# Six query column tiles by pairs of seven products, the layer input's pair operands made beside v, attention results in their own SBUF tiles

## The chip, the cores and the metric

The kernel runs on one core of a Trainium2 chip. The metric is the device time of one execution in microseconds (us). The engines are named as in the profile: PE multiplies matrices (PEld is its weight load), DVE and ACT do elementwise work and read PE's results out of PSUM, POOL does small elementwise work and issues some transfers, SP issues most transfers. All five run their own instruction list in order and wait for each other by semaphores.

## The reference

One layer of a decoder on 512 prompt tokens and 8 x 8 sample tokens, so 576 token columns in all. What matters here is the first half of the layer, up to the attention:

```python
h = _rmsnorm(x, norm1_g) * (1.0 + sc1) + sh1
proj = h @ w_in
b_gate, c_gate, xa, q, k, v, ga, gb = jnp.split(proj, cuts, axis=-1)
u = c_gate * xa
uc, new_conv = _causal_conv(u, conv_buf, conv_w)
ya = (b_gate * uc) @ w_conv_out
...
s = jnp.einsum('...qhgd,...khd->...hgqk', q, k).astype(jnp.float32) * (HEAD_DIM ** -0.5)
s = s - _alibi_slopes()[:, :, None, None] * dist[..., None, None, :, :]
s = jnp.where(valid[..., None, None, :, :], s, NEG_INF)
m = jnp.maximum(jnp.max(s, axis=-1, keepdims=True), sink)
p = jnp.exp(s - m)
p = p / (jnp.sum(p, axis=-1, keepdims=True) + jnp.exp(sink - m))
o = jnp.einsum('...hgqk,...khd->...qhgd', p.astype(v.dtype), v)
...
yb = o @ w_attn_out
mixed = jax.nn.sigmoid(ga) * ya + jax.nn.sigmoid(gb) * yb
x = x + g1 * (mixed @ w_mix_out)
```

D_MODEL is 1024. `w_in` is 1024 x 6656: 8 column tiles of 128 each for b_gate, c_gate, xa and q, 2 each for k and v, 8 each for ga and gb. There are 16 query heads of 64 in 4 groups, one group for each of 4 key heads, and the window is 128. The second half of the layer (norm, up-projection, convolution, down-projection, final norm) is not touched.

## The kernel before

**Tiles.** Activations lie with channels on the 128 partitions and the 576 tokens along the free axis: `h` is 8 tiles (k = 0 to 7) of 128 x 576. To keep float32 accuracy each operand is split in a high and a low part (ACT copies the high part, DVE subtracts it), and each product of tiles is three matmuls: high by high, high by low, low by high.

**Two ways to multiply.** `product` (L218) makes one column tile of an output: 8 k-steps x 3 passes x 2 token groups (256 and 320 tokens) = 48 matmuls of 288 columns on average, into one two-bank PSUM buffer of the pool `mm` (2 buffers). `pair_product` (L449) makes two column tiles together by Winograd's form of Strassen's scheme, on a 2 x 2 blocking of the weights (contraction halves by column tiles) and of the activations (contraction halves by token halves of 288): seven block products of 4 k-steps x 3 passes = 84 matmuls of 288 columns, in place of 2 x 48 = 96. Its parts run in this order over three PSUM regions X, Y, Z: `a0.x00` into X, `s1.n1` into Z, `s2.t2` into Y, `a1.x10` into X, `s3.n3` into Y, `s4.x11` into Z, `b1.n4` into Y. Between them ACT writes -X into Y before `s2.t2` may add to it, copies Z to a tile `p5`, and writes -Y into Z. It needs sums and differences of activation halves (`PairOperands`, L243: `sums` is four DVE operations of 128 x 288, `high` is ACT's part, `low` DVE's; the block names `n1`, `t2`, `n4`, `n3` are such sums) and of weight tiles (`pair_weights`, L394: `sums1` and `sums2` are four DVE operations of 128 x 512, then three full splits and a half one).

**Stages around the change.** k and the first query tile are multiplied while the norm is still being made. Then v is multiplied token tile by token tile (L848 to L856, 5 x 24 matmuls of 256 columns, PSUM from the pool `aux`, 4 buffers). Then query tile 1, and then a loop over `PLAIN` (L1431), six rounds called `at` 0 to 5: each multiplies a c_gate tile (`c`) and an xa tile with `product`, and DVE multiplies the two results (`pad`). Rounds 1 to 3 first multiply two query tiles each with `product`, one after the other, and `queries` (L887) takes each out of PSUM: two ACT copies `q`, two DVE operations `low`, and POOL's transfers `q<-low` that bring the other 64 partitions. Rounds 4 and 5 make the pair operands of `h` (`operands`, L1426), and their last block `n3` overwrites the second token half of four tiles of `h`, which can be done only after the last plain product, beside the first pair job (`jobs[0].before`). From then on all column tiles are multiplied by pairs (`jobs`).

**Attention.** It is a generator, `attention` (L1151), whose steps are called from `tick` inside the products at a rate of steps for each k-step (`filler`). One unit is a key head by a block of 128 queries: `prompt_scores` (PE), softmax (DVE for mask, maximum, sums and scaling; ACT for the exponentials), `prompt_turn` two units later (PE transposes, ACT copies `pt`), `prompt_values` for two units together (PE, and ACT copies into `ot`, two large tiles of four k-tiles each). A unit of a head starts only when its queries are made and 8 ticks have passed.

**Order.** PE's instructions keep the program's order from the attention on (`pinned`). DVE, ACT, POOL and SP are ordered when the program is built, by a timeline of that build, except in the stages that pin them; they then run in that order on the chip. Tiles come from a pool of 57 equal slots (`slot`); weights from 4 buffers `raw`, 5 buffers `whi` and 5 `wlo`. A new tile waits until the buffer's last reader is done.

Of the kernel before, what the change touches and what calls it, by code (L numbers as in the profile page):

```python
# [16 lines left out]
P = 128  # L17
# [16 lines left out]
CACHE_AT = 15, 16  # L34
# [38 lines left out]
def step_kernel(ctx: ExitStack, tc: tile.TileContext, ins: dict, outs: list):  # L73
# [222 lines left out]

    class BesideOperands:
# [96 lines left out]
    def pair_weights(ra, rb, moved=""):  # L394
# [22 lines left out]
        def s3_slots():  # L417
            return slot("wh", F32R, [P, 4, P]), slot("wl", F32R, [P, 4, P])
# [30 lines left out]
    def pair_product(w, x, steps, out_a0, out_a1, out_b0, out_b1):  # L449
# [3 lines left out]
        X, Z = (aux()[:, :HT] for _ in range(2))  # L453
        Y = halves(mmps())[1][:, :HT]
# [359 lines left out]
    q0 = kT.pop(0)  # L814

# [71 lines left out]
    def queries(t, ps=None):  # L887

        scale = HD**-0.5 if ps is None else 1.0
# [35 lines left out]
    queries(0, q0)  # L925
    queries(1)
    con = slot("con", shape=[P, 520])
    nc.sync.dma_start(con[:, 0:256], ins["consts"][:, CND : CND + 256])
    nd = con[:, 0:256]
# [39 lines left out]
    ot = [wp.tile([P, 4, NT], F32, tag="oh", name=nm("o"), bufs=2) for _ in range(2)]  # L969
# [86 lines left out]
    def decode_values(q, s, cV):  # L1056
# [12 lines left out]
        c = slice(512 + 32 * q, 512 + 32 * q + 32)  # L1069
        for j in range(2):  # L1070
# [12 lines left out]
            for hf in range(2):  # L1083
                src = O[HALF[hf], :P].rearrange("p (b x g t) -> p x g b t", b=4, x=2, g=2)
                dst = ot[j][:, 2 * hf : 2 * hf + 2, c]
# [45 lines left out]
    def prompt_values(parts):  # L1131
        O = aux()
        for u, (hd, i, pts) in enumerate(parts):
# [11 lines left out]
        for u, (hd, i, pts) in enumerate(parts):  # L1145
            nc.scalar.copy(
                ot[hd // 2][:, 2 * (hd % 2) : 2 * (hd % 2) + 2, i * P : i * P + P],
                O[:, 256 * u : 256 * u + 256].rearrange("p (g c) -> p g c", g=2),
            )
# [137 lines left out]
    ycv, gcv, made, made_g = {}, {}, {}, {}  # L1287
    wco, wao = ins["w_conv_out"][0], ins["w_attn_out"][0]

    class Job:  # L1290
# [9 lines left out]
        def prepare(self, moved="", late=False):  # L1300
            self.w, t = pair_weights(*self.raws, moved=moved)
# [122 lines left out]
    hp = [PairOperands(h, kp, made, xn) for kp in range(4)]  # L1424

    def operands(kp):  # L1426
        hp[kp].sums()
        hp[kp].high()
        hp[kp].low()

    for at, m in enumerate(PLAIN):  # L1431
        if at in (4, 5):
# [58 lines left out]
    def g_list(names):  # L1491
        return [g_at(int(n[0]), n[1:]) for n in names.split()]

    jobs[0].before = {2: [op.n3 for op in hp]}
    jobs[1].before = {3: [lambda: inner[6]()]}
# [10 lines left out]
        },  # L1506
        12: {0: "1third_low 3third 2third_low", 2: "3third_low"},
# [731 lines left out]
```

## Time and profile before

| | |
|---|---|
| time, median of 3 runs | 962.5 us (962.43 to 963.56) |
| profiled execution: its own time | 963.13 us |
| profiled execution: span from first to last instruction | 961.0 us |
| granted TensorE clock | 0.998 |
| v, window 52.70 to 67.30 us | 14.60 us |
| query tile 1 and the six rounds of `PLAIN`, window 67.30 to 228.40 us | 161.10 us |
| all pair jobs and the rest, from 228.40 us | 732.6 us |

The program runs on one core, so there is no second die to compare with. A window row gives, for a stretch of the span, the length, then busy time and instruction count of PE, PEld, DVE, ACT and POOL, the granted clock (1.00 is full speed), and what the transfers did. PE's matmuls overlap in their pipeline: a row that says 300 ns for one matmul is its latency, while a stream of them starts one every 0.13 us. So the length of a stretch divided by the number of its matmuls is the price of one, not the mean in the table of groups.

### The profile page before, as it was taken

What the parts mean: (1) busy time and instruction counts of PE and PEld (TensorE: products, weight loads), DVE (VectorE), ACT (ScalarE), POOL (GpSimd) and SP (SyncE); (2) the same over time, 40 slices, a digit from 0 to 9 for tenths busy, and PEclk for the clock granted to TensorE, in tenths of its full rate; (3) what the DMA queues carried; (4) which work ended last, traced back from release to release, by engine and by line L of the source; (5) the groups of instructions that cost most, each with busy time, mean ns of one, the idle gap of its engine ahead of it and who ended that gap; (6) DMA issues with size and microseconds to landing.
All of it is one profiled execution on the core that took longest, in us unless ns stands there. A gap on an engine that the chain in (4) does not pass through costs nothing.

```text
span 961.0 us, 18726 instructions
## 1 busy us (share of the span) xinstructions
PE 946.4 (98%) x7326; PEld 912.7 (95%) x7326; DVE 711.9 (74%) x1331; ACT 539.1 (56%) x1020; POOL 132.3 (14%) x309
## 2 busy tenths in 40 slices
PE   6999999999999999999999999999999999999997
PEld 5799999998999989999889999999999999999997
DVE  4656787697966767776677688995559998868874
ACT  5454665556665446875335567563226565546664
POOL 2122112201211011210001131100000001101110
PEclk9999999999999999999999999999999999999999
DMA  9985332423655767899885732332323333328542
GB/s 275 330 255 147 90 86 71 131 90 96 155 147 178 244 219 199 219 250 285 283 291 119 174 97 66 89 109 67 107 88 92 89 89 101 92 72 172 138 95 99
DMA packets 182650, 144.08 MB, mean 150 GB/s; under 512 B 7688, under 2 KB 162124, under 8 KB 182274
## 3 DMA queue, kind: packets, MB, share of 16 engines
q1 hardware_dynamic: 172546, 111.72, 38.8%
q0 software_dynamic: 9872, 30.92, 14.0%
q8 instruction: 57, 0.93, 0.4%
q14 instruction: 31, 0.25, 0.1%
q10 hardware_dynamic: 144, 0.26, 0.1%
HBM read 113.89 MB, written 12.07 MB: 131 GB/s over the span
## 4 chain that ended last, share of the span: by engine, by line
PE 95%; DMA 3%; SPq 1%; ACT 0%; DVE 0%; issue 0%; DVEq 0%
PE mm L112 55%; PE aux L112 37%; PE aux L1234 2%; DMA ad<-in_w_ada 1%; PE aux L1137 1%; DMA raw<-in_w_in 1%; SPq L497 1%; DMA q<-low 0%; ACT whi L112 0%; ACT wlo L112 0%; DVE cs L504 0%; ACT hh L112 0%; DVE hl L112 0%; DVE yo L112 0%; ACT acc L112 0%
## 5 line engine op out<-in xcount | busy, mean ns | idle before, releaser
L112 ACT ACTIVATE whi<-raw 128x1024 fp32r<-128x1024 f32 (+3 forms) x183 | 185.6, 1022 | 108.7 <-PE mm L112 51.9
L112 DVE TENSOR_TENSOR wlo<-raw,whi 128x1024 fp32r<-128x1024 f32 (+2 forms) x160 | 188.8, 1186 | 49.0 <-ACT whi L112 48.1
L112 PE MATMUL mm<-hh,whi 128*128 128x256 f32 x336 | 74.3, 302 | 0.5 <-ACT hh L112 0.5
L112 PE MATMUL mm<-hh,wlo 128*128 128x256 f32 x336 | 71.7, 295 | 0.0
L112 PE MATMUL mm<-hl,whi 128*128 128x256 f32 x336 | 70.8, 295 | 0.1
L112 PE MATMUL aux<-2h,whi 128*128 128x288 f32 (+2 forms) x232 | 68.6, 296 | 0.0
L112 PE MATMUL aux<-2l,whi 128*128 128x288 f32 (+2 forms) x232 | 68.5, 295 | 0.0
L112 PE MATMUL aux<-2h,wlo 128*128 128x288 f32 (+2 forms) x232 | 68.3, 294 | 0.0
L112 DVE TENSOR_TENSOR raw<-raw 128x512 f32<-128x512 f32 x82 | 57.5, 701 | 2.6
L112 PEld LDWEIGHTS mm<-hh,whi 128*128 128x128 f32 x336 | 55.1, 189 | 1.8 <-ACT hh L112 1.0
L112 PEld LDWEIGHTS mm<-hl,whi 128*128 128x128 f32 x336 | 55.6, 188 | 0.7 <-DVE hl L112 0.5
L112 PEld LDWEIGHTS mm<-hh,wlo 128*128 128x128 f32 x336 | 56.2, 188 | 0.0
L112 PE MATMUL aux<-hh,whi 128*128 128x288 f32 (+2 forms) x184 | 54.0, 301 | 0.0
L112 PE MATMUL aux<-hl,whi 128*128 128x288 f32 (+2 forms) x184 | 53.0, 295 | 0.0
L112 PE MATMUL aux<-hh,wlo 128*128 128x288 f32 (+2 forms) x184 | 52.9, 295 | 0.0
L112 PE MATMUL mm<-th,whi 128*128 128x288 f32 x164 | 49.2, 300 | 0.0
L112 PE MATMUL mm<-nh,whi 128*128 128x288 f32 x164 | 49.0, 299 | 0.0
L112 PE MATMUL mm<-th,wlo 128*128 128x288 f32 x164 | 48.6, 296 | 0.0
L112 PE MATMUL aux<-th,wlo 128*128 128x288 f32 x164 | 48.5, 296 | 0.0
L112 PE MATMUL aux<-th,whi 128*128 128x288 f32 x164 | 48.5, 296 | 0.0
L112 PE MATMUL mm<-nh,wlo 128*128 128x288 f32 x164 | 48.5, 296 | 0.0
L112 PE MATMUL mm<-nl,whi 128*128 128x288 f32 x164 | 48.4, 295 | 0.0
(374 smaller groups left out, 3012.3 us busy)
## 6 DMA issues: line engine op xcount, KB each, us to landing
raw<-in_w_in SPq DMA_DIRECT2D x52, 512.0 KB, 5.0
raw<-in_w_up SPq DMA_DIRECT2D x44, 512.0 KB, 3.8
ada<-in_w_ada SPq DMA_DIRECT2D x64, 256.0 KB, 5.5
wlo<-raw POOLq DMA_DIRECT2D x17, 512.0 KB, 4.6
ad<-in_w_ada SPq DMA_DIRECT2D x32, 256.0 KB, 6.6
raw<-in_w_down SPq DMA_DIRECT2D x16, 512.0 KB, 4.2
sg_dram<-sg POOLq DMA_DIRECT2D x16, 288.0 KB, 4.9
gt<-sg_dram SPq DMA_DIRECT2D x16, 288.0 KB, 6.0
```

The costliest lines, as they stand in the source:

```text
L112: done = getattr(self.engine, name)(*args, **kwargs)
L497: return tc.keep_in_program_order(nc.sync.dma_start(dst, src))
L1137: done = nc.tensor.matmul(O[HALF[par], c], vt(i - nkt + 1 + kt)[:, hd * 64 : hd * 64 + 64], pts[kt][:, par * 256 : par * 256 + 256], start ...
L1234: done = nc.tensor.matmul(ps[32 * j : 32 * j + 32, :], cT[:, k, :], cols[k][j], start=(k == 1), stop=(k == NK - 2),)
```

## The change

- **Queries by pairs.** In rounds 1 to 3 (`Q_PAIRS`) the two query tiles are made by one `pair_product` of 84 matmuls in place of two `product` calls of 48. Its weights (`q_job`) are loaded and prepared in the round before, inside that round's xa product. It takes X and Y from the pool `mm` (`apart=True`) and Z from `aux`, leaving the attention the other three `aux` buffers. The results go to two SBUF tiles `qt` (ACT copies the first halves, DVE adds `p5` for the second halves), and `queries` reads them there. The attention's rate is 0.2 steps for a tick inside a pair and 0.32 after it, in place of 0.3.
- **Operands of `h` beside v.** `EarlyOperands` makes all of `sums`, `high` and `low`, one of four k-pairs in each of v's token tiles 1 to 4. `n3` has its own tiles now, because the plain products still need `h`. The operations that rounds 4 and 5 and the first pair job had for it are gone.
- **Results in SBUF tiles of their own.** The high and low parts of the operands `n1` and `t2` (`t`) take the two large tiles that the attention's results had. The results `ot` are now eight slots, copied by 128 columns instead of two times 128 at once; the sample tokens' results go to one tile `od` and POOL copies them into `ot` before the output projection.
- **Small things.** ACT loads the exponential's table before v (`act.activation(first, ...)`). The mask constant `nd` lies in the unused half of v's last tile. The sample cache is loaded two units later (`CACHE_AT`). Some operand making of a later stage is moved by one part in `plan`.

```diff
-CACHE_AT = 15, 16
+Q_PAIRS = (1,2,3,)
+OPS_AT = 1, 2, 3, 4
+CACHE_AT = 17,18
...
+    class EarlyOperands(PairOperands):
+        def high(self):
+            made, (h0, l0), (h1, l1) = self.made, *self.x
+            if "t" not in made:
+                made["t"] = [wp.tile([P, 4, NT], F32R, tag="oh", name=nm("t"), bufs=2) for _ in range(2)]
+            self.th, self.tl = (x[:, self.kp, :] for x in made["t"])
+            act.activation(self.th, self.t, AF.Copy)
+            if self.kp % 2 == 0:
+                for n in ("n4", "n3"):
+                    made[n] = slot(n + "h", F32R), slot(n + "l", F32R)
+            a, b = slice(0, HT), slice(HT, NT)
+            at = (a, b)[self.kp % 2]
+            nh, nl = made["n4"]
+            self.nh, self.nl = nh[:, at], nl[:, at]
+            self.n3h, self.n3l = (x[:, at] for x in made["n3"])
+            act.activation(self.nh, self.r[0][:, a], AF.Copy)
+            act.activation(self.n3h, self.r[0][:, b], AF.Copy)
...
+        def all_early(self):
+            self.sums()
+            self.high()
+            self.low()
+
+        def low(self):
+            for lo, src, hi in (
+                (self.tl, self.t, self.th), (self.nl, self.r[0][:, :HT], self.nh),
+                (self.n3l, self.r[0][:, HT:], self.n3h),
+            ):
+                dve.tensor_tensor(out=lo, in0=src, in1=hi.bitcast(F32), op=ALU.subtract)
...
-        X, Z = (aux()[:, :HT] for _ in range(2))
-        Y = halves(mmps())[1][:, :HT]
+        X, Y = (halves(mmps())[1][:, :HT] if apart or n else aux()[:, :HT] for n in range(2))
+        Z = aux()[:, :HT]
...
     q0 = kT.pop(0)
+    act.activation(first, q0[:, 0:1], AF.Exp, scale=0.0)
...
+    made = {}
     for i in range(5):
+        if i in OPS_AT:
+            EarlyOperands(h, OPS_AT.index(i), made, xn).all_early()
         ps = aux()
...
         for u, (hd, i, pts) in enumerate(parts):
-            nc.scalar.copy(
-                ot[hd // 2][:, 2 * (hd % 2) : 2 * (hd % 2) + 2, i * P : i * P + P],
-                O[:, 256 * u : 256 * u + 256].rearrange("p (g c) -> p g c", g=2),
-            )
+            for g in range(2):
+                at = 256 * u + P * g
+                nc.scalar.copy(ot[2 * hd + g][:, i * P : i * P + P], O[:, at : at + P])
...
+        w = weights(kpm(w_in, 1024 + m * P), NK)
         if 1 <= at <= 3:
             key_parts(at)
-            for t in (2 * at, 2 * at + 1):
-                queries(t)
-        w = weights(kpm(w_in, 1024 + m * P), NK)
-        if at in (4, 5):
-            operands(2 * at - 8)
+            if at in Q_PAIRS:
+                qt = [slot("qt") for _ in range(2)]
+                filler[1] = .2
+                pair_product(q_job.w, made["op"], {}, *copy_outs(qt), True)
+                filler[1] = .32
+            for n in range(2):
+                queries(2 * at + n, qt[n] if at in Q_PAIRS else None)
...
         w = weights(kpm(w_in, 2048 + m * P), NK)
-        if at in (4, 5):
-            operands(2 * at - 7)
         steps = {}
+        if at + 1 in Q_PAIRS:
+            q_job = Job(w_in, Q0 + (2 * at + 2) * P, None, None)
+            q_job.load()
+            fs = [f for x in q_job.prepare("").values() for f in x]
+            for k, n in [(0, 2), (1, 1), (2, 1), (3, 1), (4, 2), (5, 1), (6, 1), (7, 1)]:
+                steps[k], fs = fs[:n], fs[n:]
...
-    jobs[0].before = {2: [op.n3 for op in hp]}
-    jobs[1].before = {3: [lambda: inner[6]()]}
+    jobs[1].before = {4: [lambda: inner[6]()]}
...
     def part_o(n):
         for k in range(len(o), n):
-            o.append(split_slot(ot[k // 4][:, k % 4, :], "o"))
+            nc.gpsimd.tensor_copy(out=sv(ot[k]), in_=od[0][:, k, :])
+            o.append(split_slot(ot[k], "o"))
```

In the built order, names carry a number for each buffer. The first place is ACT around the first pair, between the xa product of round 0 (`mm_1006` before, `mm_1062` now) and what follows it. `whi` of round 1's weights, `y` and `kh` are the convolution's first tap and the next key head; the rows `s,den` are the exponentials of one attention unit; `mm_1191` is X, `mm_1192` is Y, `aux_1193` is Z. Before:

```order
L984 ACTIVATE s_1025,den_1045<-s_1025,nmx_1041 128x128 x2
L984 ACTIVATE s_1026,den_1045<-s_1026,nmx_1041 128x128 x2
L990 ACTIVATE es_1046<-es_1046 128x4
L112 ACTIVATE whi_1588<-raw_1586 128x1024
L112 ACTIVATE y_1096<-pad_1089,parT 128x592
L112 ACTIVATE kh_1100<-kT_663 64x512
L112 ACTIVATE whi_1702<-raw_1700 128x1024
L896 ACTIVATE q_1230<-mm_1112 64x512
```

Now:

```order
L114 ACTIVATE whi_1179<-raw_1177 128x1024
L114 ACTIVATE y_1173<-pad_1166,parT 128x592
L114 ACTIVATE kh_1183<-kT_663 64x512
L1028 ACTIVATE s_1091,den_1111<-s_1091,nmx_1107 128x128 x2
L1028 ACTIVATE s_1092,den_1111<-s_1092,nmx_1107 128x128 x2
L114 ACTIVATE mm_1192<-mm_1191 128x288
L1034 ACTIVATE es_1112<-es_1112 128x4
L114 COPY p_1194<-aux_1193 128x288
L114 ACTIVATE aux_1193<-mm_1192 128x288
```

The exponentials of the first attention unit moved behind the weight split, `y` and `kh`, and the pair's -X into Y stands behind all of these.

The second place is DVE while v and then query tile 1 are multiplied. `tw` and the changed `xn` are the operands' sums, `t`, `n4l` and `n3l` their low parts, `wlo_1055` and `wlo_1003` are the same low part of round 0's xa weights. Before:

```order
L112 TENSOR_TENSOR wlo_854<-raw_851,whi_853 128x1024
L112 TENSOR_TENSOR wlo_942<-raw_939,whi_941 128x1024
L112 TENSOR_TENSOR wlo_1003<-raw_1000,whi_1002 128x1024
L112 TENSOR_TENSOR wlo_1109<-raw_1106,whi_1108 128x1024
L112 TENSOR_TENSOR wlo_1243<-raw_1240,whi_1242 128x1024
L112 TENSOR_TENSOR kl_835<-kT_663,kh_834 64x512
```

Now:

```order
L114 TENSOR_TENSOR wlo_994<-raw_991,whi_993 128x1024
L114 TENSOR_TENSOR tw_713<-xn_304 128x288
L114 TENSOR_TENSOR tw_713<-xn_469,tw_713 128x288
L114 TENSOR_TENSOR xn_304<-xn_304,xn_469 128x288
L114 TENSOR_TENSOR xn_304<-xn_469,tw_713 128x288
L114 TENSOR_TENSOR wlo_1055<-raw_1052,whi_1054 128x1024
L114 TENSOR_TENSOR t_719<-tw_713,t_718 128x576
L114 TENSOR_TENSOR n4l_722<-xn_304,n4h_721 128x288
L114 TENSOR_TENSOR n3l_724<-xn_304,n3h_723 128x288
L114 TENSOR_TENSOR tw_756<-xn_306 128x288
```

The sums of the first k-pair come before round 0's xa weights and the rest follows them, ahead of the key's and the queries' low parts (`kl`, `low`).

More of the change, by code (lines that the diff above doesn't have):

```diff
@@ L417, in s3_slots @@
         def s3_slots():
+            if not narrow:
+                return [x[:, 0:4, :] for x in tiles()]
             return slot("wh", F32R, [P, 4, P]), slot("wl", F32R, [P, 4, P])
@@ L885, in key_parts, with queries @@
         KS[hd] = kh, kl
-    def queries(t, ps=None):
-        scale = HD**-0.5 if ps is None else 1.0
+    def queries(t, ps=None, scale=HD**-0.5):
         if ps is None:
@@ L968, in step_kernel @@
     pinned.append(pe)
-    ot = [wp.tile([P, 4, NT], F32, tag="oh", name=nm("o"), bufs=2) for _ in range(2)]
+    ot = []
+    od = []
     def softmax_steps(s, n, sinks, nsinks, w):
@@ L1068, in decode_values @@
         yield False
-        c = slice(512 + 32 * q, 512 + 32 * q + 32)
+        c = slice(32 * q, 32 * q + 32)
+        if not od:
+            od.append(slot("od", shape=[P, NK, 64]))
         for j in range(2):
@@ L1132, in prompt_values @@
         O = aux()
+        while len(ot) < 2 * parts[-1][0] + 2:
+            ot.append(slot("ot"))
         for u, (hd, i, pts) in enumerate(parts):
@@ L1300, in prepare @@
         def prepare(self, moved="", late=False):
-            self.w, t = pair_weights(*self.raws, moved=moved)
+            self.w, t = pair_weights(*self.raws, moved=moved, narrow=self.outs is not None)
             order = {0: "sums1 ah al", 1: "bh bl", 3: "dh dl sums2", 4: "ch", 5: "cl"}
@@ L1422, in step_kernel @@
     jobs += [Job(wco, m * P, made_g, lambda m=m: conv_outs(m)) for m in range(0, NK, 2)]
[L1424 to L1429, printed above, removed]
     for at, m in enumerate(PLAIN):
```

22 lines of the change are left out of this document (13 added, 9 removed), and 2 rows, old and new, of the table plan.

## The prediction

> **What bounds the kernel now.** I read the page's first part and its chain that ended last, then the windows by stage, then the chain in order of time.
>
> ```profile
> span 961.0 us, 18726 instructions
> PE 946.4 (98%) x7326; PEld 912.7 (95%) x7326; DVE 711.9 (74%) x1331; ACT 539.1 (56%) x1020; POOL 132.3 (14%) x309
> PE 95%; DMA 3%; SPq 1%; ACT 0%; DVE 0%; issue 0%; DVEq 0%
> ```
>
> The last chain is 95% PE work. Busy time alone would not prove that, as matmuls overlap, but the chain says that PE seldom waited. The windows show it for the stages that the change touches:
>
> ```profile
> 52.70:67.30 14.60, 14.60 (x125) 14.60 (x124) 4.28 (x4) 7.24 (x16) 0.54 (x1) 1.00 0.93 260
> 67.30:228.40 161.10, 160.78 (x1256) 153.55 (x1254) 121.53 (x327) 93.25 (x248) 28.46 (x62) 1.00 0.36 103
> ```
>
> The first row is v, the second query tile 1 and the six rounds. PE is busy for all but 0.32 us of 175.7 us, at full granted clock (1.00). DVE is busy for 125.8 us (4.28 + 121.53), 72%, ACT for 100.5 us. So here a matmul that is taken away shortens the kernel by its full price, as long as DVE and ACT deliver in time; a faster DVE or ACT brings nothing.
>
> **The price of the matmuls.** The chain in order of time has two plain products without anything between them, and the steady pairs of the up-projection:
>
> ```profile
> 67.35 12.67 PE mm L112 x96
> ...
> 741.71 3.17 PE aux L112 x24
> ...
> 752.84 3.19 PE aux L112 x24
> ...
> 763.98 3.18 PE aux L112 x24
> ```
>
> Two products take 12.67 us for 96 matmuls, 0.132 us each. A piece of 24 `aux` matmuls is the first two parts of a pair, X and Z, so from one such piece to the next is one pair: 11.13 us (752.84 - 741.71) and 11.14. That is 84 matmuls at 0.1325 us, with nothing lost between the parts. One pair for two products saves 12.67 - 11.13 = 1.54 us, three save 4.62 us. The attention's own PE work is the same in both kernels, and in the built order the last prompt values stand just before the first pair job in both, so nothing of it is pushed into a later stage.
>
> **The operands beside v.** Their parts and those of the weights have these rows (groups from 52 to 245 us, the last three from 228 to 450 us; behind the bar busy us, then the mean of one in ns):
>
> ```profile
> L112 DVE TENSOR_TENSOR wlo<-raw,whi 128x1024 fp32r<-128x1024 f32 x25 | 30.5, 1223 | 18.0 <-ACT whi L112 17.8
> L112 ACT ACTIVATE whi<-raw 128x1024 fp32r<-128x1024 f32 x26 | 27.3, 1057 | 40.9 <-PE mm L112 25.9 <-issue 6.2 <-DMA raw<-in_w_in 3.9
> L112 DVE TENSOR_TENSOR tl<-tw,th 128x576 fp32r<-128x576 f32 x4 | 3.0, 751 | 3.5 <-ACT th L112 3.3
> L112 DVE TENSOR_TENSOR raw<-raw 128x512 f32<-128x512 f32 x4 | 2.8, 690 | 0.1
> L112 ACT ACTIVATE th<-tw 128x576 fp32r<-128x576 f32 x4 | 2.7, 683 | 0.9 <-PE aux L112 0.9
> L112 DVE TENSOR_TENSOR tw<-xn,tw 128x288 f32<-128x288 f32 x4 | 1.8, 454 | 0.1
> L112 ACT ACTIVATE nh<-xn 128x288 fp32r<-128x288 f32 x4 | 1.7, 430 | 0.0
> L1146 ACT COPY o<-aux 128x256 f32<-128x256 f32 x16 | 5.2, 375 | 9.5 <-PE aux L1137 9.5
> ...
> L112 ACT ACTIVATE wh<-s 128x512 fp32r<-128x512 f32 x18 | 11.2, 623 | 0.0
> L112 ACT ACTIVATE mm<-aux 128x288 f32<-128x288 f32 x18 | 7.2, 397 | 12.3 <-PE aux L112 12.3
> L112 ACT COPY p<-aux 128x288 f32<-128x288 f32 x18 | 7.0, 390 | 3.0 <-PE aux L112 2.7
> ```
>
> Sums, 16 x 0.454 = 7.3 us, and low parts, 4 x 0.751 + 8 x 0.454 = 6.6 us, make 13.9 us on DVE; high parts, 4 x 0.683 + 8 x 0.430 = 6.2 us on ACT. The cover is v and query tile 1 with the next PE work, until 86 us:
>
> ```profile
> 67.30:86.00 18.70, 18.70 (x145) 18.70 (x144) 10.40 (x25) 9.70 (x21) 8.09 (x16) 1.00 0.71 196
> ```
>
> DVE is idle there for 10.3 us in v and 8.3 us after it, 18.6 us, ACT for 16.4 us. The operands fit, and the first pair needs them at about 87 us. Behind them in DVE's order are the low parts of the key and of two query tiles; until the last of these is done, the xa product cannot have its PSUM buffer.
>
> ```profile
> 61.27 1.23 DVE L112 TENSOR_TENSOR wlo<-raw,whi 128x1024 fp32r<-128x1024 f32 x1 [5.33 <-ACT whi L112]
> ...
> 78.76 0.22 DVE L907 TENSOR_SCALAR qX<-mm 64x64 f32<-64x64 f32 x1
> ...
> 87.42 0.69 DVE L112 TENSOR_TENSOR pad<-mm,c 128x512 f32<-128x512 f32 x1 [0.51 <-PE mm L112]
> 88.03 0.86 DVE L994 TENSOR_SCALAR s<-s,den 128x128 f32<-128x128 f32 x4
> 88.81 0.22 DVE L112 TENSOR_TENSOR pad<-mm,c 128x64 f32<-128x64 f32 x1
> ```
>
> Before, the last of them ended at 78.98 us and the product began at 80.02 (67.35 + 12.67). Now four sums fill DVE's 5.33 us of idle time, and from 61.27 on stand two splits (2.4 us), the rest of the operands (13.9 - 1.8) and five low parts of about 0.69 with some small ones (4.2): 80.0 us by full durations. Successive DVE operations overlap by about 0.08 us (`pad` at 87.42 lasts 0.69, the next starts at 88.03); over some 30 of them that is 2.4 us, so 77.6. Between 0 and 0.1 us for PE; I take 0. ACT's table load goes from the attention to a time when ACT waits for a transfer; PE waits for it in neither place.
>
> **The weights and the results.** Each pair adds on DVE 4 x 0.690 (sums) + 0.690 (half low part; no row of this stage, so the same size) + 1.223 (three low parts for two), 4.7 us, and 2 x 0.454 for the second halves of `qt`. On ACT it adds 1.057 + 0.623, and 5 x 0.39 (-X, -Y, `p5`, two copies), 3.6 us. `n3` comes from the pair job: 4 x 0.45 us on each. The results' copies go from 16 x 0.375 to 32 copies of half the width. Half width is not in this row; between 0.19 (proportional) and 0.375, they add 0 to 6 us on ACT, and I take 3. DVE then has 125.8 + 3 x 5.6 + 1.8 = 144.4 us in 175.7 - 4.6 = 171.1 us, 84%; ACT 100.5 + 10.9 + 1.8 + 3 = 116.2, 68%. Both still fit, but DVE has 27 us of slack in place of 50. Averages do not settle it; the hand-overs do.
>
> **The hand-over inside a pair.** This is the one new place where PE waits for ACT at short notice. Y takes the `mm` buffer in which the xa product has just ended. PE may add `s2.t2` to Y only when DVE has read that product (`pad`), and ACT has written -X there. Until then PE has X, 8 score matmuls and Z. Rows of round 0 on ACT, and eight score matmuls from the chain:
>
> ```profile
> 85.93 0.39 ACT L984 ACTIVATE s<-s,nmx 128x128 f32<-128x128 f32 x1
> ...
> 87.20 1.06 ACT L112 ACTIVATE whi<-raw 128x1024 fp32r<-128x1024 f32 x1 [0.70 <-ACT es L990]
> 89.12 0.79 ACT L112 ACTIVATE y<-pad,parT 128x592 f32<-128x592 f32 x1 [0.86 <-DVE pad L112]
> 89.94 0.63 ACT L112 ACTIVATE kh<-kT 64x512 fp32r<-64x512 f32 x1
> ...
> 88.18 0.94 PE aux L112 x8
> ```
>
> PE's cover is 12 x 0.1325 + 0.94 + 12 x 0.1325 = 4.1 us. ACT's list in that time, by the built order of the first pair: `whi` 1.06 (its buffer is freed by the xa product's end), `y` 0.79, `kh` 0.63, four exponentials of 128 at 0.39, -X 0.40: 4.4 us. `pad` itself, 0.69 + 0.22 with nothing between its two parts now, is done within `whi`. PE waits 0.3 us. The second pair has the same list, the third no exponentials ahead. So 0.6 us in all. The bounds: 0 if the overlap of successive ACT instructions is worth 0.3 us; and up to 1.5 us for each pair if DVE comes to `pad` one low part (1.223 us) later than I think, 4.5 us in all. I take 0.6, near the low end, since DVE's order puts no long operation between the xa product's end and `pad`.
>
> The Trainium skill speaks against this (Perfetto Trace Analysis, Matmuls): independent matmul groups should rotate through different PSUM banks, so that emptying one overlaps the next group. A pair that takes both `mm` buffers gives up that rotation once for each pair. In this trace the steady pairs, which take one of their three regions from there, lose nothing (11.13 us above); what the rule would cost here is in the third rival.
>
> **The queries' transfer.** Before, head 3 was the only PE wait in the six rounds:
>
> ```profile
> PE aux L112 <- DMA q<-low: 0.3, 1, 0.3
> ...
> L896 ACT ACTIVATE q<-mm x14: 572/590/596, 74.4 to 176.3; 64x512 fp32r<-64x512 f32 x14
> L899 DVE SCALAR_TENSOR_TENSOR low<-mm,q x14: 672/688/695, 77.3 to 177.9; 64x512 fp32r<-64x512 f32 x14
> ...
> DMA to landing us min/median/max: 2.2/2.7/6.9
> ...
> 178.24 4.48 DMA q<-low
> ```
>
> From ACT's last copy at 176.3 to the landing at 182.7 are 6.4 us. Now both tiles of a head come at once, 4 x 0.590 on ACT and 4 x 0.688 on DVE in place of half of each, about 2.6 us more: 9.0 us. In the built order PE has between the pair and the head's first scores a c_gate product and 18 to 24 matmuls of the xa product (66 to 72 x 0.132 = 8.7 to 9.5 us), and 16 to 21 of the attention's, at 0.94 / 8 each 1.9 to 2.5 us: 11 us or more. That covers it, and the old wait of 0.3 us goes.
>
> **The sum.** Against the profiled execution's own 963.13 us (span 961.0, 2.1 us around it): -4.62 (matmuls) - 0.3 (old wait) + 0.6 (hand-over) = -4.3, so 958.8. That execution lies 0.6 us above the median of the three runs, 962.5; by the median 958.2. I say 958.5 us.
>
> **The rivals.** The third needs two rows of the softmax:
>
> ```profile
> L984 ACT ACTIVATE s<-s,nmx 128x256 f32<-128x256 f32 x50 | 24.9, 501 | 4.5 <-DVE nmx L978 2.8 <-DVE den L992 1.6
> L975 DVE TENSOR_REDUCE nmx<-s 128x2 f32<-128x512 f32 x26 | 17.0, 678 | 0.0
> ```
>
> 1. *Half of it is given back.* DVE at 84% is late at `pad` or at the weights by about 0.8 us a pair, within the bound above: 3 x 0.8 - 0.6 = 1.8 us more, 960.3. For it: the slack halves. Against: the list above has only 0.3 us missing.
> 2. *The queries come late.* If one head's transfer meets the worst landing (6.9, 4.2 above the median) and the softmax queued ahead of it takes 2 us more, that head waits 4 us: 962.5, no change that can be told. Against: 11 us of cover.
> 3. *Slower: the hand-over decides.* ACT comes to -X only behind a softmax unit that itself waits for DVE. Its price for a pair is four wide exponentials in place of the narrow ones of my list (4 x 0.501, 0.4 us more) and two maxima (2 x 0.678) and a low part (1.223) on DVE before them: 0.3 + 0.4 + 1.4 + 1.2 = 3.3 us at most. Past 1.54 us for each pair the change loses; at 2.3 us each the time is -4.6 + 6.9 = +2.3, 964.8. This is the mechanism by which the Trainium skill's rule on PSUM rotation would come true. For it: in two pairs exponentials stand ahead of -X. Against: in DVE's built order both maxima stand ahead of `pad` and only one operation of 128 x 4 between it and those exponentials, so their inputs are there while ACT is still at `y`.
> 4. *It does nothing,* because PE is not the bound: against it stands the window with 0.32 us of PE idle.
>
> **How the numbers follow.** Forecast (957.2 to 960) 0.64; rival 1 (to 961.6) 0.16; rival 2 with rival 4, 0.10; rival 3, 0.10. The three runs of before span 1.1 us; a change of 0.2%, 1.9 us, is about what can be told from none. Faster than 960.6: the forecast and most of rival 1, 0.78. Within 0.2%: 0.13. Slower: 0.09. The low end is the full saving with no new wait, 957.6, less 0.4 for the spread; the high end takes in rival 1, 961.5.
>
> **What would show it.** Right: the window from v's end to the first pair job is about 4.5 us shorter, with some 1220 PE instructions, PE idle in it under 1 us; each pair with its score matmuls taken out lasts 11.1 to 11.5 us; PE's waits name ACT's -X (`mm<-mm`) with a few tenths, and not `q<-low`. Wrong: PE idle of over 1.5 us beside a pair, a wait for `wlo` or for `q<-low`, or windows after 228 us that changed their length, which nothing here accounts for.

## The result and the profile after

| | before | after |
|---|---|---|
| median of 20 runs | 962.9 us | 960.96 us |
| ratio, 95% interval | | 0.9981 (0.9974 to 0.9988) |
| profiled execution: own time / span | 963.13 / 961.0 us | 960.62 / 958.8 us |

The change is 1.9 us faster; 4.3 was forecast. The sign was right, the size was not. The page of the changed kernel begins so:

```profile
span 958.8 us, 18738 instructions
PE 944.6 (99%) x7290; PEld 909.4 (95%) x7290; DVE 725.8 (76%) x1355; ACT 549.1 (57%) x1058; POOL 132.9 (14%) x317
PE 90%; DMA 3%; ACT 2%; issue 2%; DVE 1%; SPq 1%; POOL 0%; POOLq 0%; ACTq 0%; DVEq 0%
```

PE's share of the last chain fell from 95% to 90%: the chain now goes through ACT and DVE in places. The windows say where. I divided both kernels at the same matmuls: the stage from the first matmul of v to the first of the first pair job, and the jobs from there to the first of the output projection. (The window that ended at 228.40 us before the change leaves out the last 1.6 us of the last plain product.) Before, then after:

```profile
52.76:230.00 177.24, 176.92 (x1390) 169.69 (x1389) 127.14 (x332) 102.03 (x266) 29.01 (x63) 1.00 0.41 115
230.00:451.69 221.69, 221.69 (x1776) 211.80 (x1775) 164.25 (x262) 142.00 (x262) 37.48 (x59) 1.00 0.74 204
```

```profile
52.27:226.53 174.26, 173.95 (x1354) 165.40 (x1352) 144.21 (x363) 114.21 (x305) 30.04 (x64) 1.00 0.42 117
226.53:448.96 222.43, 222.20 (x1777) 211.91 (x1775) 160.96 (x255) 140.02 (x260) 37.17 (x66) 1.00 0.73 201
```

The stage with the pairs lost 36 matmuls, as written, but only 2.98 us. The jobs behind it, where I had put nothing, are 0.74 us longer. So the question for the experiments: what took 1.3 us of the stage and 0.74 us of the jobs, while PE reads as busy for all but 0.3 and 0.2 us of them?

PE's waits of the changed kernel in these two stretches (what waited for what, total, times, longest) give almost nothing:

```profile
PE mm L114 <- ACT mm L114: 0.3, 1, 0.3
PE mm L114 <- ACT aux L114: 0.2, 1, 0.2
```

A busy row hides it, because a matmul that starts late behind another one's tail is no idle time. Distances between starts show it. Around the end of the second pair, PE in order of time:

```profile
130.90 0.30 PE L114 MATMUL aux<-hl,whi 128*128 128x288 f32 x1
131.04 0.30 PE L114 MATMUL aux<-hh,wlo 128*128 128x288 f32 x1
131.26 1.94 PE L1185 MATMUL aux<-pt,V 128*64 128x256 f32 x14
133.13 0.40 PE L114 MATMUL mm<-n4h,whi 128*128 128x288 f32 x1
133.37 0.29 PE L114 MATMUL mm<-n4l,whi 128*128 128x288 f32 x1
...
136.51 0.65 PE L1185 MATMUL aux<-pt,V 128*64 128x256 f32 x2
```

`aux<-pt,V` are the attention's value matmuls, 128x64 in place of 128x128. From 131.04 to the first of them are 0.22 us, not 0.13; from 133.13 to the next of the pair 0.24, not 0.13. And the group is cut: 14 records at 131.26, the last two at 136.51, when the next product has begun. Another group is cut in six and six, the first six here and the others at 186.06, among head 3's scores (`aux<-kh,q` and `aux<-kl,q`):

```profile
182.04 0.28 PE L114 MATMUL aux<-kl,q 128*128 128x128 f32 x1
182.24 1.08 PE L1185 MATMUL aux<-pt,V 128*64 128x256 f32 x6
183.25 0.33 PE L114 MATMUL aux<-kh,q 128*128 128x128 f32 x1
```

The group table shows the price of the same 112 records (busy us, then mean ns), before and after:

```profile
L1137 PE MATMUL aux<-pt,V 128*64 128x256 f32 x112 | 13.9, 387 | 0.0
```

```profile
L1185 PE MATMUL aux<-pt,V 128*64 128x256 f32 x112 | 15.1, 388 | 0.0
```

1.2 us more for the same work, so about 0.6 us in this row for each of the two cuts; the late starts of the matmuls around them come on top. Where the cuts fall matters too. A matmul leaves two records, and the matmuls of the two halves of the 128 columns run side by side, so the records start in twos: 131.53 and 131.54, 131.75 and 131.75, a two every 0.21 us. Both cuts separate such a two: the records at 132.61, 132.82, 136.51 and 136.78 each stand alone. So a piece of 2 records takes as long as one of 4 in these traces (0.58 us to the next other matmul), 6 as long as 8 (1.01), 14 as long as 16 (1.87 and 1.88). The Trainium skill says of this (TensorEngine Tiling (Array Packing), Tiling Modes, Key Properties) that changing the tiling mode drains the engine. The late starts agree with that; the price is from the rows.

### The profile page after: what moved, and what is told of

Same layout as the page of the kernel before. It is cut to its first block, busy times and chain, and to the rows that moved or that the text cites. A ratio compares the mean times of both kernels' runs of the same rounds, so it can differ in the third digit from the quotient of the medians.

```text
span 958.8 us, 18738 instructions
## 1 busy us (share of the span) xinstructions
PE 944.6 (99%) x7290; PEld 909.4 (95%) x7290; DVE 725.8 (76%) x1355; ACT 549.1 (57%) x1058; POOL 132.9 (14%) x317
## 4 chain that ended last, share of the span: by engine, by line
PE 90%; DMA 3%; ACT 2%; issue 2%; DVE 1%; SPq 1%; POOL 0%; POOLq 0%; ACTq 0%; DVEq 0%
PE mm L114 50%; PE aux L114 37%; PE aux L1281 2%; PE aux L1185 2%; DMA ad<-in_w_ada 1%; SPq L538 1%; DMA wlo<-raw 1%; DMA raw<-in_w_down 1%; ACT whi L114 1%; DMA x<-in_x_prompt 1%; ACT wlo L114 0%; ACT xh L114 0%; ACT sg L114 0%; ACT nh L114 0%; DVE tl L114 0%
## 5 line engine op out<-in xcount | busy, mean ns | idle before, releaser
L114 PE MATMUL mm<-hh,whi 128*128 128x256 f32 (+2 forms) x264 | 60.6, 303 | 0.5 <-ACT hh L114 0.5
L114 PE MATMUL mm<-hh,wlo 128*128 128x256 f32 (+2 forms) x264 | 58.3, 295 | 0.0
L114 PE MATMUL aux<-hh,whi 128*128 128x288 f32 (+1 forms) x196 | 57.5, 300 | 0.0
L114 PE MATMUL mm<-hl,whi 128*128 128x256 f32 (+2 forms) x264 | 57.4, 295 | 0.1
L114 PE MATMUL aux<-hl,whi 128*128 128x288 f32 (+1 forms) x196 | 56.5, 295 | 0.0
L114 PE MATMUL aux<-hh,wlo 128*128 128x288 f32 (+1 forms) x196 | 56.4, 295 | 0.0
L114 PE MATMUL mm<-fh,whi 128*128 128x256 f32 x224 | 48.0, 296 | 0.4 <-DVE rt L114 0.4
L114 PE MATMUL mm<-fh,wlo 128*128 128x256 f32 x224 | 47.9, 295 | 0.0
L114 PE MATMUL mm<-fl,whi 128*128 128x256 f32 x224 | 47.8, 295 | 0.0
L114 PEld LDWEIGHTS aux<-2h,whi 128*128 128x128 f32 x232 | 43.7, 188 | 0.0
```

The costliest lines, as they stand in the source:

```text
L114: done = getattr(self.engine, name)(*args, **kwargs)
```

## The experiments

The theories: A, cuts of value matmuls; H, hand-overs inside the pairs; R, the rest of the change; and later P, SBUF tiles: the 57 slots are all in use, so a new tile waits for the last reader of an old one. Ratios are to the kernel before, on the same chip. DVE, ACT, POOL and SP are ordered anew when an edited kernel is built, so no run changes one thing alone.

**Values kept together.** The value matmul that reads the newest `pt` goes first, the others have priority behind it.

```diff
-        for u, (hd, i, pts) in enumerate(parts):
+        for u, (hd, i, pts) in reversed(list(enumerate(parts))):
...
-                kt, par = n // 2, n % 2
...
+                kt, par = nkt - 1 - n // 2, n % 2
+                with tc.high_priority() if done else nullcontext():
...
```

> The changed kernel, with the attention's value matmuls of two units kept together on PE: the newest turned tile comes first, the rest have priority over the pair's matmuls. In the changed kernel two of the eight groups are cut in two (14 + 2 and 6 + 6 records), so PE goes in and out of this kind of matmul ten times. Theory A (each going in and out costs about 0.5 us: in the traces the first such matmul, the last one and the matmul behind it start 0.14, 0.19 and 0.1 us late): eight groups again, 0.9 to 1.1 us less than the change, so -2.8 to -3.0 us against the kernel before; the matmuls named aux<-pt,V take 13.3 us in place of 14.4 in the stage. Rival H (the time is lost in hand-overs, the cuts only fill a wait of PE): the same -1.9 us, and the pair's b1.n4 waits instead for DVE's qt.

Measured: 960.08 us, ratio 0.9972 (0.9960 to 0.9984), -2.8 us. The interval overlaps the change's, so the median alone does not decide. The trace does: the group is back at 13.9 us, and a wait stands where the second cut was:

```profile
L1190 PE MATMUL aux<-pt,V 128*64 128x256 f32 x112 | 13.9, 386 | 0.0
```

```profile
PE aux L114 <- DMA q<-low: 1.1, 1, 1.1
```

So A is right about the cuts, and one of them had filled a wait for head 3's queries. That is why the stage itself is only 0.1 us shorter than in the changed kernel (174.14 us). From start to start that wait costs 1.29 us; without it the stage would be 172.9. So in the stage the two cuts cost about 1.4 us (174.26 - 172.9), 0.7 us each.

**No pairs.** `Q_PAIRS = ()`, all else as changed.

> The changed kernel with no query tile made by a pair: all six by plain products, the operands of h beside v, the results' own tiles, the moved operand making of a later stage kept. Theory A and H (what was lost is lost beside and inside the pairs; the rest is hidden): 0 +- 0.5 us against the kernel before, stage from v to the first pair job 177.0 to 177.5 us. Rival R (the rest of the change costs 1 to 1.5 us of its own, in the jobs behind 227 us and in the copies): +1.0 to +1.5 us, the jobs' stretch 220.7 us long as in the change, in place of 220.0.

Measured: 970.41 us, ratio 1.0081 (1.0064 to 1.0098), +7.6 us: neither theory. The profiled execution took 974.13 us, 3.7 us above the median; in it the stage is 181.5 us and the jobs 227.7 us. The chain of this run names the first cause:

```profile
72.43 0.38 DVE xn L114
...
72.88 5.39 DMA con<-in_consts
...
78.78 0.34 POOL q L947
...
79.62 7.04 DMA q<-low
```

A constant's load starts only when DVE has done with `xn`, POOL stands behind that load, and head 0's queries land at 86.66. Before, PE began these scores at 82.34 us and did not wait in them; here it waits 2.35 and 0.53 us. A second wait, 2.8 us for DVE's `g`, follows in the jobs, behind a transfer `wl<-s`. After each of the two long waits the granted clock is 0.50 for a while (to about 90.2 us, and from 261 to 268 us), and a matmul starts every 0.24 us in place of 0.13. Waits and slow matmuls together make up what this trace has lost, so this run says nothing of R's price. It led to theory P.

**The later stage's plan put back** (`plan` 11 and 12 and `jobs[1].before`).

> The changed kernel with the later stage's operand making (plan 11 and 12) and the modulation step of the second job put back where they were before. Rival R, in the part that the profile shows (PE starts 0.16 and 0.34 us late at 406.7 and 410.1 us, in the first pair of the convolution's output, for ACT): these two are gone, the jobs' stretch is 0.5 us shorter, -2.4 us against the kernel before. Theories A and H: -1.9 us, no change, and PE waits there or elsewhere as before.

Measured: 960.72 us, ratio 0.9976 (0.9968 to 0.9985). Stage 174.9 (with a wait of 0.4 us for `q<-low`), jobs 223.0 us, longer, not shorter, and PE still starts late at the same pair (0.33 us at 409.24, 0.42 at 412.58). This part of R falls.

**X from a single bank** (`apart=False` in the three pairs).

> The changed kernel with the three query pairs' X in the pool of single banks, as in all other pairs, and only Y in the pool of two-bank buffers: Y is then the buffer that the c_gate product had, which is free early, so that ACT's -X does not wait for DVE to read the xa product. Theory H: the waits at the start of s2.t2 (0.57 us in the first pair, 0.16 in the second) are gone, -2.6 us against the kernel before. Theory A: at most these 0.7 us, and the attention has two single banks in place of three, which costs about as much or more: -1.5 to -2.2 us, with PE waits for aux<-... inside the pairs.

Measured: 961.12 us, ratio 0.9981 (0.9970 to 0.9992). The pairs' start is unchanged: `s2.t2` begins 0.6 us behind the start of Z's last matmul, as in the changed kernel. So the PSUM buffer is not what -X waits for.

**Sample scores later** (two `yield False` ahead of `decode_scores`).

> The changed kernel with two empty steps of the attention ahead of the sample tokens' first scores. In the changed kernel DVE's first operation on these scores waits until 236.5 us, though they are ready at 233.7, because its tile is one that the first pair job reads up to 236.4 (PE mm<-n3l,wh); PE then waits 0.2 us twice for the single banks at 236.8 and 237.2. Theory P (the 57 tiles are all in use, so new tiles wait for old readers): these two waits go, 0.4 to 0.5 us less in the jobs' stretch (222.0 us in place of 222.4 from the first pair job to the first matmul of the output projection), -2.3 to -2.4 us against the kernel before. Rival (the scores only collide with the weights' preparation there, and do so later too): the stretch stays 222.4 us, -1.9.

Measured: 968.42 us, ratio 1.0057 (1.0045 to 1.0070), +5.5 us. The waits at 236.8 went, as P said, and a larger one came. The chain of this run:

```profile
247.32 0.64 ACT wl L114
...
248.26 5.73 DMA wl<-s
...
254.01 0.47 DVE g L114
```

In the built program the tile `g` of the second job is the one whose old content, a weight sum `s`, the transfer `wl<-s` still reads. ACT came to `wl` late, behind the exponentials that the edit had moved there; DVE waited 2.80 us for the tile and PE 4.3 us for DVE. Behind that wait the granted clock was 0.50 until about 257.6 us, with a matmul every 0.24 us, and PE waited 1.5 us more for a transfer `ada` at 381 us. My number missed; the cause of the large wait is P's, at another place, to which the moved sample attention brought it.

**A control and the test of P.** In both, `y` of columns 1, 2, 4 and 5 is written over column 0's, so tiles become free and the own `y` of these four columns is left out.

```diff
...
-            u, parT[:, 64 + m : 65 + m], parT[:, 72 + m : 73 + m], parT[:, 80 + m : 81 + m], stT[:, :, :, m]
+            u, parT[:, 64 + m : 65 + m], parT[:, 72 + m : 73 + m], parT[:, 80 + m : 81 + m], stT[:, :, :, m],
+            ycv[0] if m in (1, 2, 4, 5) else None,
```

> A control: the kernel before with four of the convolution's tiles y (columns 1, 2, 4, 5) written over that of column 0, so that these columns get a wrong y, and one to four tiles more are free from the second round on. Theory P says that only the changed kernel is short of tiles: 0 to -0.5 us against the kernel before (at most its wait for head 3's queries, 0.53 us, goes). Rival (free tiles help any order by about the same): -1 us or more.

> The changed kernel with the value matmuls kept together, and with four of the convolution's tiles y written over that of column 0 (these columns get a wrong y), so that one to four tiles more are free from the second round on. With the values together alone PE waited 1.29 us for head 3's queries at 181.4 us, and 0.41 us at 236.7 for DVE's tile of the sample scores. Theory P (both wait for a tile): both gone, stage from v to the first pair job 172.8 us in place of 174.1, jobs' stretch 222.0 us, -4.2 to -4.5 us against the kernel before. Rival Q (the queries are late because DVE and ACT have too much to do behind the pair): the stage stays 174.1 us, -2.8 to -3.2 us.

Measured: the kernel before with free tiles 962.82 us, ratio 0.9996 (0.9987 to 1.0005): free tiles bring it nothing. The changed kernel with values together and free tiles 958.70 us, ratio 0.9956 (0.9943 to 0.9970), -4.2 us. The interval overlaps that of the values kept together, so the windows decide:

```profile
51.59:224.36 172.77, 172.45 (x1355) 165.05 (x1353) 144.86 (x366) 114.18 (x305) 32.17 (x66) 1.00 0.45 123
224.36:446.11 221.75, 221.60 (x1777) 211.85 (x1776) 159.87 (x252) 140.32 (x260) 36.27 (x64) 1.00 0.72 199
```

The stage is 172.8 as P said, and the jobs, forecast at 222.0, are back at the length before, 221.7. Rival Q falls as far as the amount of work goes, since DVE and ACT have the same work as in the changed kernel. At head 3's queries, ACT's copies `q` after, then here:

```profile
168.58 1.29 ACT L940 ACTIVATE q<-qt 64x512 fp32r<-64x512 f32 x2 [1.14 <-DVE qt L114]
...
172.07 0.63 ACT L940 ACTIVATE q<-qt 64x512 fp32r<-64x512 f32 x1
174.10 0.63 ACT L940 ACTIVATE q<-qt 64x512 fp32r<-64x512 f32 x1 [1.40 <-DVE low L943]
```

```profile
165.78 1.27 ACT L940 ACTIVATE q<-qt 64x512 fp32r<-64x512 f32 x2
169.74 1.29 ACT L940 ACTIVATE q<-qt 64x512 fp32r<-64x512 f32 x2
```

In the changed kernel the fourth copy waits 1.40 us for DVE's `low`, though `low` is no input of it. In the built program it is the wait for a tile that `low` was the last to read. But on the chip this wait had slack. DVE, after:

```profile
172.66 1.40 DVE L943 SCALAR_TENSOR_TENSOR low<-qt,q 64x512 fp32r<-64x512 f32 x2
174.10 1.28 DVE L1019 TENSOR_REDUCE nmx<-s 128x2 f32<-128x512 f32 x2
175.29 1.22 DVE L114 TENSOR_TENSOR wlo<-raw,whi 128x1024 fp32r<-128x1024 f32 x1
176.43 1.40 DVE L943 SCALAR_TENSOR_TENSOR low<-qt,q 64x512 fp32r<-64x512 f32 x2
```

DVE is never idle here, and the fourth copy was done at 174.73, before DVE came to its low part. So on the chip the order of DVE's list made the queries late: two maxima and a `wlo` stand ahead of the last two low parts. In the run with free tiles the order is another one, and these low parts end 6.5 us after the pair (174.75 and 168.30) in place of 7.6 (177.83 and 170.22). That the full pool made the old order is likely, as one tile less in each pair also took the wait away (below), but another order with the pool as full was not tried. At the sample scores it is a wait on the chip. DVE, after and here:

```profile
236.55 0.87 DVE L1092 SCALAR_TENSOR_TENSOR s<-con,aux 128x256 f32<-128x256 f32 x2 [5.46 <-PE mm L114]
```

```profile
231.51 0.87 DVE L1092 SCALAR_TENSOR_TENSOR s<-con,aux 128x256 f32<-128x256 f32 x2 [2.60 <-PE aux L114]
```

After, DVE waits for a matmul of the pair, `mm`, which is not the scores' own bank; with free tiles it waits for the scores themselves, `aux`. What it costs shows on PE: from the matmul ahead of them on, start to start, the matmuls of the sample scores take 3.53 us in the jobs before, 4.11 us after and 3.29 us here. That is 0.58 of the 0.74 us.

**The price of a cut by itself.** The kernel before, seven groups cut in two.

```diff
...
+                O = prompt_values([(0, *units[n - 4], pts.pop(n - 4))])
             if 2 <= n <= len(units) + 1:
                 pts[n - 2] = prompt_turn(units[n - 2][1], s.pop(n - 2))
+            if n >= 4 and n % 2 == 0:
+                prompt_values([(1, *units[n - 3], pts.pop(n - 3))], O)
```

> The disputed price by itself: the kernel before, with seven of its eight groups of value matmuls cut in two on purpose (one unit ahead of the next transposes, the other behind them); the number of matmuls and of the attention's steps stays. Theory A (going into and out of these matmuls costs 0.45 to 0.5 us each time): 7 x 0.45 to 0.5 = +3.1 to +3.5 us against the kernel before, nearly all of it in the stage from v to the first pair job. Rival (the late starts in the trace overlap with something and cost little): +0.5 us or less.

Measured: 969.57 us, ratio 1.0070 (1.0058 to 1.0082), +6.5 us, twice the forecast; the profiled execution took 967.67 us. In it the stage grew by 5.7 us, of which 2.9 are two waits that my edit brought (both halves share one PSUM bank, and the second waits for the copy of the first):

```profile
PE aux L1137 <- ACT o L1145: 2.9, 2, 2.0
```

The other 2.8 us are at most 0.4 us for each cut. So a cut costs: 0.4 us here, 0.7 in the changed kernel. The difference is where they fall. Here every piece has 4 or 8 records, so no two is separated; there both cuts leave single records, which take 0.21 us more on either side of the cut.

**Versions that compute all.** `p5` takes the second half of the first result tile, which the pair writes last.

```diff
-        p5 = slot("p5")[:, :HT]
+        p5 = slot("p5")[:, :HT] if keep is None else keep[:, HT:]
```

The first has this for the query pairs only, and two empty steps ahead of the sample scores:

> A candidate that computes all: the changed kernel with the value matmuls kept together, the query pairs' p5 put into the second half of the first result tile (one tile less in use, its sum is then made in place), and two empty steps ahead of the sample tokens' first scores. In its built order the last copy of head 3's queries waits for transfers that were started earlier, not for DVE's low part. Theory P: PE's wait for head 3's queries 0 to 0.6 us, no wait at the sample scores, -3.7 to -4.3 us against the kernel before. Rival Q: the wait of 1.29 us stays, -3.2 us.

Measured: 968.52 us, ratio 1.0057 (1.0044 to 1.0069), as with the two steps alone, and with the same waits in the jobs: 4.3 us for DVE's `g`, 2.0 for `ada`. In the stage P's forecast held: no wait for head 3's queries, 172.9 us. The next run has it for the branch, gate and inner pairs too, without empty steps:

> Computes all: the changed kernel with the value matmuls kept together and p5 of the query, branch, gate and inner pairs in the second half of their first result tile, so one tile less is in use in each pair. The empty steps ahead of the sample scores are left out, as they cost 4.5 us at 250 us, where DVE's g waited for a tile that a transfer of weights still read. Theory P: stage from v to the first pair job 172.9 us, the sample scores still wait 0.4 us (their tile is read by the first pair job, as in the changed kernel), jobs' stretch 222.4 us, -3.4 to -3.9 us against the kernel before. Rival Q (queries late for another reason than tiles): stage 174.1, -2.8.

Measured: 959.52 us, ratio 0.9963 (0.9951 to 0.9975), -3.6 us, the best version that computes all; its interval just touches the change's. Stage 173.0, jobs 221.9 us, 0.5 less than forecast; the wait at the sample scores is there, as expected. With one empty step more:

> As the run with p5 in place, and with one empty step ahead of the sample tokens' first scores. In its built order the sample scores and the second job's g no longer wait for tiles that weights or the first pair job still read. Theory P: the wait at the sample scores gone too, no wait of DVE's g at 250 us, jobs' stretch 222.0 us, -3.8 to -4.3 us against the kernel before. Rival (the place of the sample attention is what counts, not the tiles): 4 us or more are lost beside the second job again, 0 to +1 us.

Measured: 961.62 us, ratio 0.9988 (0.9980 to 0.9997). Theory P's number failed: the jobs are 224.6 us, not 222.0. Starts are 0.6 and 1.5 us late at 245 and 249 us, the second behind DVE's `g`, so the loss beside the second job is still there, only smaller. This time `g` waits for no tile. In DVE's list the two later taps of the convolution's `y` now stand ahead of it (behind it in the run before), and DVE waited 2.46 us for ACT's `y` at the first of them. So a free tile alone does not settle this place; the rival, that the place of the sample attention counts, is right in kind, at half its price. And with `kh` moved behind the pair:

> As the run before it, and the copy kh of the next key head (0.63 us on ACT) moved behind the query pair. Theory H for what is left at s2.t2: ACT's list ahead of -X is the cause (whi, y, kh, four exponentials), not the PSUM buffer, since X in a single bank left the wait as it was. Without kh the wait of 0.47 us in the first pair is gone: 0.5 us less in the stage, -4.3 to -4.8 us against the kernel before. Rival: the wait stays 0.4 to 0.5 us, since the exponentials take the free place; no gain over the run before.

Measured: 963.18 us, ratio 1.0002 (0.9994 to 1.0011). The gain I looked for is there: the chain goes through the first pair without ACT.

```profile
88.97 1.19 PE mm L114 x9
90.16 1.58 PE aux L114 x12
91.74 4.78 PE mm L114 x36
```

X ends, Z takes 1.58 us, and Y starts at once. Without its score matmuls this pair lasts 11.12 us, in place of 11.70 in the changed kernel. But head 3's queries are late again (1.2 us for `q<-low`), and the second job's 2.1 us stay.

## Why the prediction came out as it did

| step of the sum | forecast | trace |
|---|---|---|
| 36 matmuls fewer | -4.62 | -4.75 (worked out, 36 x 0.132) |
| head 3's wait | -0.3 | -0.5 (start to start), but paid for by a cut |
| hand-over of -X | +0.6 | +0.7 |
| value matmuls | 0 | +1.4 to +1.5 (1.2 in their row) |
| stage, not assigned | | about +0.1 |
| jobs behind 227 us | 0 | +0.74 |

**The matmuls: right.** With the cuts and the tile waits taken away the stage is 172.8 us, 4.5 less than before; my terms gave 4.3.

The time itself, 960.96 us, lies in the band that I gave to the first rival (up to 961.6), but that is luck. DVE was late at neither `pad` nor the weights; what took the time is in the table's rows of the value matmuls and of the jobs.

**Operands, weights, results: right.** I had 18.6 us more on DVE and 15.7 on ACT. From the first of v to the first pair job DVE went from 127.1 to 144.2 us, 17.1 more, and ACT from 102.0 to 114.2, 12.2 more; the copies of half width cost less than I took. PE waited for nothing between v and the first pair.

**The hand-over: right in mechanism, and in size as a sum.** The chain through the first pair:

```profile
88.22 1.19 PE mm L114 x9
89.41 0.39 PE aux L114 x3
89.80 1.16 ACT s L1028 x6
90.96 0.30 ACT mm L114
```

ACT had `whi`, `y`, `kh` and the exponentials ahead of -X, the list of the forecast. PE lost 0.47 us there and 0.1 at the restart, 0.16 in the second pair, nothing in the third; I had 0.3 in each of the first two. Moving `kh` took it away, another bank for X did not: what was late was ACT's own list. The third rival, 3.3 us a pair at most, did not come. The Trainium skill's rule on PSUM rotation (Perfetto Trace Analysis, Matmuls), by which it would have come true, has no price in this place. With the score, value and transpose matmuls taken out the three pairs last 11.70, 11.61 and 11.38 us; 11.1 to 11.5 was the sign of being right, so the first two missed it by 0.1 to 0.2.

**The value matmuls: the step that failed first.** I wrote that "the attention's own PE work is the same in both kernels" and looked only at where its last values stand. Number and work are the same; their places are not. The first value matmul of a group is not pinned, so the scheduler moved it forward into gaps that it saw (beside `b1.n4`, and at head 3's scores) and gave PE back to the pair in the middle. Each cut is one more way in and out, and these two also separate records that would have run side by side. Both cuts stand in the order that was built, where I looked for the end of the values alone. With the groups whole the stage is 1.4 us shorter once the wait of 1.29 us is taken off, and 1.5 us shorter in the run with free tiles.

**The queries' transfer: mis-sized.** I had 9.0 us from copies to landing and 11 us of cover. After, the pair's last sum was done at about 168.3 us and POOL's last issue was at 178.4, landing up to 4.2 us later: 14 us. PE came to head 3's scores at 181.53 us, 13.2 us after that sum. I had added durations of four copies and four low parts; what I left out is the rest of DVE's list, which was never idle: three `wlo` of 1.22 us, 1.4 us for masks and 1.3 us for maxima stand between its parts. This is the outcome of the second rival, late queries, at about 1.3 us instead of 4 when the values are kept whole. Its mechanism held only in part: softmax work of another unit was in the list, but no transfer met the landing of 6.9 us, 4.2 was the longest.

**Nothing for the jobs behind 228 us: failed.** The sum has no term for them: I looked at their instructions and not at the tiles. The change holds own tiles for `n3`, the eight results, `qt` and `od`, and it holds `n4` from v on; against that only the eight tiles `th` and `tl` and the mask's `con` left it. With the pool full, a later tile waits for a reader that has nothing to do with it. That shows at the sample scores, 0.58 us, and the jobs return to 221.7 us with free tiles. The Trainium skill says (Perfetto Trace Analysis, Optimization Strategy) that the same gap repeating on an engine can mean too little SBUF for the next tile. The cause is the one found here, but no gap repeats: they are single ones of 0.4 to 4.3 us on PE, and the edits here moved them.

The rest of the difference between the two traces is not the change's. v began 0.49 us earlier, but over all runs of this study it began anywhere from 51.1 to 53.5 us. The second half is 0.5 us longer, 0.4 of it a wait for DVE's `rt` that was 0 to 1.6 us in runs with the same code there. Open is whether it was the full pool that put DVE's low parts so late in the built order, and 0.25 us at the first pairs of the convolution's output, where ACT's -X is late; putting the plan back did not remove that.

## What to carry to other kernels

When a change adds tiles to a pool that is already full, the cost need not stand beside the change: it can be a later instruction that waits for a stranger's last read. Look in the built order for the waits that no operand explains, check in the trace whether each one has slack, and free tiles before moving steps: here one tile less in each pair, with the groups kept whole, gave 1.7 us more than the change alone (-3.6 and -1.9), and one empty step in the wrong place took 2.1 us back. And where groups of matmuls of another shape are left to float, count how many groups there are and where they are divided, not only how many matmuls.

## What the runs showed of the hardware

Going into and out of matmuls of 64 output columns between full ones cost at most 0.4 us each time where the pieces were whole (seven cuts, 2.8 us), and 0.7 us where a cut separated two records that start together (two cuts, 1.4 us). A busy row of PE does not show these late starts.

The first full matmul behind such a group, and the first behind PE's wait for -X, was followed by the next after 0.24 us in place of 0.13 (133.13 to 133.37 us; from 91.31 us on).

After v began, PE's waits of up to 1.99 us (the run with seven groups cut) left the granted clock at 1.00. Behind waits of 2.35 and 2.82 us (no pairs) and 4.3 us (sample scores later) it was 0.50 for 3.5 to 7 us, and matmuls of 288 columns started every 0.24 us in place of 0.13.
